# Wide products for eight chunk pairs, grouped seam splits and a narrower last column block in a one-core fp32 transformer layer

## Chip, core and metric

One core of a Trainium2 chip runs the whole layer as one program. The metric is the device time of one execution in microseconds; the lower the better. The engines named below are TensorE (PE, with its weight loads PEld), VectorE (DVE), ScalarE (ACT), GpSimd (POOL) and SyncE (SP, which issues most DMAs).

## What is computed

The reference is one decoder layer on 256 tokens of width 1024, in fp32. Each of its four blocks normalises its input by RMS, adds the normalised output to the residual x, and has its own gains:

```
x = x + 0.5 * rmsnorm(swiglu(rmsnorm(x), w_gate, w_up, w_down))      # FFN 1, inner width 2816
proj = rmsnorm(x) @ w_in                       # q, k, v (8 heads of 64) and 512 pool channels
y = concat(attention(q, k, v), pool(p_in)) @ w_out                    # the mixer
x = x + rmsnorm(y)
c = cross_attention(rmsnorm(x) @ wq, rmsnorm(mem) @ wkv) @ wo         # 256 memory rows, 4 heads of 256
x = x + rmsnorm(c)
x = x + 0.5 * rmsnorm(swiglu(...))                                    # FFN 2
```

With 256 tokens the attention of the mixer is plain causal attention with a linear bias; the pool branch takes trailing means over 2, 4, 8 and 16 positions.

## The kernel before

**Products.** Every large product is made from three products of rounded halves. A weight block `w` of 128x128 is split into `hi` (a rounding copy on ACT, L76) and `lo = w - hi` (DVE, L77), and the activations are split in the same way, `X[:, k, :256]` being the high part of feature block k for all 256 tokens and `X[:, k, 256:]` the low part. The product is `lo*Xhi + hi*Xhi + hi*Xlo`.

- `pair` (L206) makes two output chunks of 128 features by 256 tokens in the two halves of one PSUM bank. It calls `product` (L176) eight times per chunk, once per k: three matmuls of 256 columns (L179 to L181), each with a weight load of its own.
- `gate_up` (L593), used in the two FFNs, makes a chunk in a bank of its own. Per k it runs `lo` over the 256 columns of Xhi into the second half of the bank (L603) and `hi` over all 512 columns of X into the whole bank (L606). The two halves are then added: ACT copies the second half to `cmb` (L611), DVE adds it to the first half (L612) into an SBUF tile.
- `group` makes four chunks at once, k by k: four `lo` matmuls (L233) and then for each chunk L238 and L240. `rows` makes token-major rows of 512 columns (L266 to L268).

**Weights.** All weight blocks stand in DRAM in the order of use, eight blocks to a unit (1 MB for two units). `Weights.get` (L125) hands out blocks; when a new unit u begins it first makes the splits (L76, L77) of all units up to u + LEAD, with LEAD = 4, unless the list `pace` says another number for this unit. A split made further ahead is queued earlier on ACT and DVE.

**Order.** PE runs in program order everywhere. Between `seam(True)` and `seam(False)` all engines run in program order; elsewhere a scheduler at build time orders ACT, DVE, POOL and SP. The two seams of the change are those from FFN 1 to the mixer and from the mixer to the cross-attention, both by `row_end` (L378). A seam runs, in this order:

1. `products` (L391): sets `pace`, takes the last three weight units, finishes the row products of both token halves (`row_sums`), adds the first half to the residual, and transposes it on PE into two banks.
2. `middle` (L416): the root of the second half; eight high parts (`x_hi`, ACT, L384) of the first half; residual additions (L357); eight low parts (`x_lo`, DVE, L388).
3. Two filler chunks (a `pair` of the memory keys K), each followed by `turned(i)` (L433): four transposes of the second half into one bank, then for each of the four blocks `x_hi` and `x_lo`.
4. `group` on the new activations (four chunks, four units: G0 to G3, two k per unit). Its `before(j)` adds the evacuation of the filler pair (`k_flush`) at k = 1 and squares for the next norm at k = 2, 4, 6 and 7.

The old pace is four units ahead for the first two units of `products`, three for its third, two for the two fillers and for G0, and three for G1 and G2.

**After the first seam (mixer).** `pair` of k (chunks 4, 5), the root `x_root` and its broadcast `x_spread` (PE L292), `q_out` (L1000, multiplies the four q chunks and the k chunk pair by the norm), `pair` (6, 7), scores of heads 0 to 3, `pool_pair(3)` (L1010), scores of heads 4 to 7, `pool_pair(1)`, four steps of `rows` for v with the transposes of the attention probabilities (`self_turn`, L787 to L790) and the pool products (`pool_out`, L830) between them, then a K pair. `pool_windows` begins with the multiply L813 on DVE, which reads the pool chunk's bank; POOL then makes the sums. Softmax of the scores runs on DVE and ACT.

**After the second seam (cross-attention).** Two `pair`s of wq (chunks 4 to 7), a K pair, `k_flush`, and then scores against the memory with the v rows between them.

**PSUM.** Eight banks: two under the name `small`, six under `accum`. Each `pair` takes one `accum` bank until what it feeds has read it; a `self_turn` of heads 0 to 3 takes one each, the v rows two, a `pool_out` one each.

**Tail.** `last_rows` (L718) finishes FFN 2. For the second token half the first 256 output columns go by PE: x times the identity (L736) plus y times a diagonal of the norm (L741), copied out by ACT (L745) and stored by ACT's queue (L748). The columns 512 to 1023 and 256 to 511 go by DVE (L753) and SP (L746, L747).

Of the kernel before, what the change touches and what calls it, by code (L numbers as in the profile page):

```python
# [15 lines left out]
P = 128  # L16
# [126 lines left out]
def build(nc, io, tiles_only=False):  # L143
# [53 lines left out]
    def chunk(name, X, nk, col, evac, alloc=accum):  # L197
# [5 lines left out]
            evac(ps)  # L203
        pr.add(run, [(name, k * P, col) for k in range(nk)])

    def pair(name, X, cols, done, between=None, alloc=accum):  # L206

        names = [name] * 2 if isinstance(name, str) else name
        box = []

        def half(s):
            def run():
                if s == 0:
                    box.append(alloc())
                for k in range(ND):
                    product(halves(box[0])[s], st["w"].get(), st[X][:, k, :], s == k == 0, k == ND - 1)
                if s:
                    done(box[0])
# [159 lines left out]
    def row_end(parts, ks, weights, factor, nxt, pre, fillers):  # L378
# [4 lines left out]
        def x_hi(t, c):  # L383
            nc.scalar.activation(st[nxt][:, c, t * P:(t + 1) * P], st["turned", t, c], AF.Copy, scale=gain(pre, c))  # L384
# [5 lines left out]

        def products():  # L391
            st["w"].pace = [(LEAD, None)] * (LATE - 1)
            st["w"].pace += [(LEAD - 1, None)] + [(LEAD - 2, None)] * 3 + [(LEAD - 1, None)] * 2 if fillers else []
            ws = [st["w"].get(UNIT) for _ in ks]
            st["w"].flush()
            st["ys"] = keep([P, 2, D], "y")
            r = row_root(row_sums(parts, ks, ws, 0, factor))
            st[nxt] = xsplit()
            st["xsum"] = tmp([P, 2, 2], "xsum")
            for d in HALVES:  # L400
                row_add(0, d, r)
            box["later"] = []
            between = {} if fillers else {(1, i): lambda i=i: turn_first(i) for i in range(2)}
            box["sums"] = row_sums(parts, ks, ws, 1, factor, box["later"], between)
            if fillers:
                for i in range(2):
                    x_turn(0, range(4 * i, 4 * i + 4), small)
# [25 lines left out]
        def turned(i):  # L433
            def run():
                cs = range(4 * i, 4 * i + 4)
                x_turn(1, cs, accum)
                for c in cs:
                    x_hi(1, c)
                    x_lo(1, c)
            return run  # L440

# [148 lines left out]
    def ffn(n, X, before, aside, last):  # L590
        wg, wu, wd = (f"ffn{n}_w_{s}" for s in ("gate", "up", "down"))

        def gate_up(f, done):  # L593

            box = []

            def half(s):
                def run():
                    ps = (accum, small)[s]()
                    for k in range(0, ND, 2):  # L600
                        ws = [st["w"].get() for _ in range(2)]
                        for i, (hi, lo) in enumerate(ws):
                            nc.tensor.matmul(ps[:, S:], lo, st[X][:, k + i, :S], start=k == i == 0, stop=False,  # L603
                                             skip_group_check=True)
                        for i, (hi, lo) in enumerate(ws):
                            nc.tensor.matmul(ps, hi, st[X][:, k + i, :], start=False, stop=k + i == ND - 1,  # L606
                                             skip_group_check=True)
                    if s == 0:
                        box.append(st["ffn"].tile([P, 2, S], F32, name="gu", bufs=6))
                    c = tmp([P, S], "cmb")  # L610
                    nc.scalar.copy(c, ps[:, S:])  # L611
                    nc.vector.tensor_tensor(box[0][:, s, :], ps[:, :S], c, op=ALU.add)  # L612
                    if s:
                        done(box[0])
                return run
            return [(half(s), [(w, k * P, f * P) for k in range(ND)]) for s, w in enumerate((wg, wu))]
# [101 lines left out]
    def last_rows(parts, ks, weights):  # L718
        def run():
            ws = [st["w"].get(UNIT) for _ in ks]  # L720
            st["w"].flush()
            ys = st["ys"] = keep([P, 2, D], "y")
            xt = st["xt"]
            for t in range(2):
                o = io["out"][t * P:(t + 1) * P, :]
                later = [] if t else None
                s = row_sums(parts, ks, ws, t, 0.5, later)
                if t == 0:
                    r = row_root(s)
                    for i in range(4):  # L730
                        row_out(t, quarter(i), r)
                    for a, b in ((0, 512), (512, 1024)):
                        nc.sync.dma_start(o[:, a:b], ys[:, t, a:b])
                    continue
                turn = accum()
                nc.tensor.matmul(turn[:, :S], st["ident"], xt[:, t, quarter(0)], start=True, stop=False,  # L736
                                 skip_group_check=True)
                r = row_root(s, later[0])
                diag = tmp([P, P], "diag", bufs=1)
                nc.scalar.activation(diag, st["ident"], AF.Copy, scale=r)  # L740
                nc.tensor.matmul(turn[:, :S], diag, ys[:, t, quarter(0)], start=False, stop=True,  # L741
                                 skip_group_check=True)
                for d in (slice(512, 1024), quarter(1)):
                    row_out(t, d, r)
                nc.scalar.copy(ys[:, t, quarter(0)], turn[:, :S])  # L745
                nc.sync.dma_start(o[:, 512:], ys[:, t, 512:])  # L746
                nc.sync.dma_start(o[:, S:512], ys[:, t, S:512])  # L747
                nc.scalar.dma_start(o[:, :S], ys[:, t, :S])  # L748
        pr.add(run, weights)

    def row_out(t, d, r):
# [212 lines left out]
        pr.add = add  # L964
        return out

    K = [collect(pair, "xa_wkv", "xs_mem", [c * P, (c + 1) * P], k_out(c)) for c in range(0, ND, 2)]
    V = [s for half in range(2)
         for s in rows("xa_wkv", "xs_mem", D + 512 * half, xv_done(512 * half))]
    vv = rows("w_in", "xs_mix", D, v_done)  # L970
# [22 lines left out]

    group("w_in", "xs_mix", [c * P for c in range(4)], lambda ps: held.update(q=ps), before=run)
    seam(False)
    pair("w_in", "xs_mix", [4 * P, 5 * P], lambda ps: held.update(k=ps), lambda: side(x_root))
    table(AF.Exp)
    side(x_spread)

# [10 lines left out]
    def pool_pair(g):  # L1010
        def done(ps):
            for i in (g, g - 1):
                pool_in(i)(halves(ps)[g - i])
                pool_windows(i)
        pair("w_in", "xs_mix", [(12 + g) * P, (11 + g) * P], done)
    side(q_out)
    pair("w_in", "xs_mix", [6 * P, 7 * P], lambda ps: scaled_pair("qk", 6, ps))
    side(self_scores, 0, small)
    side(self_scores, 1, accum)
    pool_pair(3)  # L1020
# [59 lines left out]
    side(xq_root)  # L1080
    table(AF.Exp)
    for c in (4, 6):
        pair("xa_wq", "xs_xa", [c * P, (c + 1) * P], lambda ps, c=c: split_pair(st["xs_q"], c, ps))
    k = K.pop(0)
    pr.add(*k[0])
    pr.add(*k[1])
# [139 lines left out]
```

## Time and profile before

| | |
|---|---|
| median of 3 runs | 573.33 us (573.03 to 573.44) |
| the profiled execution's own time | 573.43 us |
| its span, first to last instruction | 571.6 us |
| mean granted PE clock | 0.998 |
| PE busy | 562.0 us, 98% of the span |
| DVE, ACT busy | 408.0 us (71%), 343.6 us (60%) |
| POOL busy | 15.7 us |
| DMA | 107.02 MB, mean 187 GB/s |

The span leaves about 1.8 us of the execution's time outside. Times of rows are microseconds from the start of the span. A row of the timeline is start, duration, engine, line, operation, output<-inputs, shape, count of merged instructions, and in brackets the idle time before it and what ended it. Consecutive matmuls overlap in their recorded durations, so the rate of PE is read from the distance between starts.

### The profile page before, as it was taken

How to read it: one execution, taken by the hardware profiler on the slowest of the kernel's cores; microseconds unless marked ns; L12 is line 12 of the kernel's file. 1: busy time of each engine (PE TensorE's matmuls, PEld its weight loads, DVE VectorE, ACT ScalarE, POOL GpSimd, SP SyncE). 2: the span in 40 equal slices, each digit the busy share in tenths (PEclk: the TensorE clock that was granted, in tenths of full speed). 3: DMA queues.
4: the chain of work that ended last, by engine and by line, in shares of the span. 5: the costliest groups of instructions: out<-in, count | busy, mean ns of one | idle time of the engine just before them, and what ended most of it. 6: DMA issues, size and time to landing. Idle time of an engine off the chain costs nothing.

```text
span 571.6 us, 8375 instructions
## 1 busy us (share of the span) xinstructions
PE 562.0 (98%) x3264; PEld 492.7 (86%) x3264; DVE 408.0 (71%) x661; ACT 343.6 (60%) x615; POOL 15.7 (3%) x34
## 2 busy tenths in 40 slices
PE   9999999999999999999999999999999999999996
PEld 8888888888888989988889988888888888888884
DVE  5989667777875678985478666466976776767644
ACT  7788665556556585884369456358754555555542
POOL 0000000000000000550000000000000000000000
PEclk9999999999999999999999999999999999999999
DMA  8996866555541378262077644332866556564102
GB/s 298 365 357 236 303 242 214 198 211 163 215 163 61 109 282 309 75 221 75 0 257 294 225 147 148 108 113 77 337 218 215 162 208 201 171 215 159 66 0 73
DMA packets 29255, 107.02 MB, mean 187 GB/s; under 512 B 2080, under 2 KB 2976, under 8 KB 28832
## 3 DMA queue, kind: packets, MB, share of 16 engines
q1 hardware_dynamic: 28640, 106.01, 52.3%
q10 hardware_dynamic: 576, 0.48, 0.3%
q8 instruction: 25, 0.41, 0.3%
q14 instruction: 14, 0.11, 0.1%
HBM read 105.44 MB, written 1.05 MB: 186 GB/s over the span
## 4 chain that ended last, share of the span: by engine, by line
PE 89%; DVE 6%; ACT 2%; DMA 2%; issue 1%; SPq 0%; DVEq 0%; ACTq 0%
PE sm L606 12%; PE acc L606 12%; PE acc L306 10%; PE acc L304 10%; PE acc L305 9%; PE acc L603 6%; PE sm L603 6%; PE acc L179 3%; PE acc L180 3%; PE acc L181 3%; DVE wlo L77 2%; PE acc L266 2%; PE acc L268 2%; PE acc L267 2%; DMA wraw<-w 2%; DVE xs L388 1%
## 5 line engine op out<-in xcount | busy, mean ns | idle before, releaser
L77 DVE TENSOR_TENSOR wlo<-wraw,whi 128x1024 fp32r<-128x1024 f32 x184 | 224.9, 1230 | 71.4 <-ACT whi L76 70.3
L76 ACT CAST whi<-wraw 128x1024 fp32r<-128x1024 f32 x184 | 191.7, 1052 | 48.6 <-PE acc L306 37.2
L606 PE MATMUL acc<-xs,whi 128*128 128x512 f32 x320 | 100.5, 395 | 0.0
L606 PE MATMUL sm<-xs,whi 128*128 128x512 f32 x320 | 100.5, 395 | 0.0
L603 PEld LDWEIGHTS acc<-xs,wlo 128*128 128x128 f32 x320 | 60.0, 188 | 14.5 <-DVE wlo L77 0.8
L603 PEld LDWEIGHTS sm<-xs,wlo 128*128 128x128 f32 x320 | 59.8, 188 | 13.8
L306 PE MATMUL acc<-whi,h 128*128 128x512 f32 x176 | 68.6, 390 | 0.2 <-DVE h L195 0.2
L304 PE MATMUL acc<-whi,h 128*128 128x512 f32 x176 | 68.6, 390 | 0.0
L305 PE MATMUL acc<-wlo,h 128*128 128x512 f32 x176 | 68.5, 389 | 0.0
L603 PE MATMUL acc<-xs,wlo 128*128 128x256 f32 x320 | 63.0, 278 | 0.6 <-DVE wlo L77 0.6
L603 PE MATMUL sm<-xs,wlo 128*128 128x256 f32 x320 | 63.2, 279 | 0.0
L606 PEld LDWEIGHTS sm<-xs,whi 128*128 128x128 f32 x320 | 48.7, 189 | 0.0
L606 PEld LDWEIGHTS acc<-xs,whi 128*128 128x128 f32 x320 | 48.7, 189 | 0.0
L179 PE MATMUL acc<-xs,wlo 128*128 128x256 f32 x160 | 46.1, 288 | 0.0
L180 PE MATMUL acc<-xs,whi 128*128 128x256 f32 x160 | 45.2, 283 | 0.0
L181 PE MATMUL acc<-xs,whi 128*128 128x256 f32 x160 | 45.2, 283 | 0.0
L611 ACT COPY cmb<-acc 128x256 f32<-128x256 f32 x40 | 14.9, 372 | 49.7 <-PE acc L606 49.7
L611 ACT COPY cmb<-sm 128x256 f32<-128x256 f32 x40 | 14.9, 372 | 49.2 <-PE sm L606 48.9
L306 PEld LDWEIGHTS acc<-whi,h 128*128 128x128 f32 x176 | 33.0, 188 | 7.7 <-DVE h L195 0.9
L305 PEld LDWEIGHTS acc<-wlo,h 128*128 128x128 f32 x176 | 33.0, 188 | 7.0
L304 PEld LDWEIGHTS acc<-whi,h 128*128 128x128 f32 x176 | 33.0, 188 | 7.0
L179 PEld LDWEIGHTS acc<-xs,wlo 128*128 128x128 f32 x160 | 30.6, 191 | 0.3
(196 smaller groups left out, 883.5 us busy)
## 6 DMA issues: line engine op xcount, KB each, us to landing
wraw<-w SPq DMA_DIRECT2D x91, 1024.0 KB, 4.9
post<-post SPq DMA_DIRECT2D x4, 512.0 KB, 5.2
wraw<-w SPq DMA_DIRECT2D x7, 256.0 KB, 5.7
wraw<-w SPq DMA_DIRECT2D x2, 512.0 KB, 7.1
y<-memt SPq DMA_DIRECT2D x1, 1024.0 KB, 5.2
y<-mem SPq DMA_DIRECT2D x1, 1024.0 KB, 7.0
xt<-xt SPq DMA_DIRECT2D x1, 1024.0 KB, 6.8
out_dram<-y SPq DMA_DIRECT2D x3, 256.0 KB, 2.1
```

What stands on the lines that cost most here:

```text
L76: self.nc.scalar.copy(hi, raw)
L77: eng.tensor_tensor(lo, raw, hi.bitcast(F32), op=ALU.subtract)
L179: nc.tensor.matmul(o, lo, X[:, :S], start=first, stop=False, skip_group_check=True)
L180: nc.tensor.matmul(o, hi, X[:, :S], start=False, stop=False, skip_group_check=True)
L181: nc.tensor.matmul(o, hi, X[:, S:], start=False, stop=last, skip_group_check=True)
L266: nc.tensor.matmul(box[t], a, hi, start=k == 0, stop=False)
L304: nc.tensor.matmul(o, a, hi, start=first, stop=False, skip_group_check=True)
L305: nc.tensor.matmul(o, a, lo, start=False, stop=False, skip_group_check=True)
L306: nc.tensor.matmul(o, b, hi, start=False, stop=last, skip_group_check=True)
L603: nc.tensor.matmul(ps[:, S:], lo, st[X][:, k + i, :S], start=k == i == 0, stop=False, skip_group_check=True)
L606: nc.tensor.matmul(ps, hi, st[X][:, k + i, :], start=False, stop=k + i == ND - 1, skip_group_check=True)
L611: nc.scalar.copy(c, ps[:, S:])
```

## The change

Five edits.

1. `wide`, `wide_chunk` and `wide_pair` are new. `wide_chunk` is the body of `gate_up` taken out: per two k it runs two `lo` matmuls of 256 columns and two `hi` matmuls of 512, then ACT copies the second half to `cmb` and DVE adds. `wide_pair` makes two such chunks, each in an `accum` bank of its own, into one SBUF tile `wide` of 512 columns with one buffer, and hands that tile to what read the bank before.
2. Eight `pair`s become `wide_pair`s: K chunks (2, 3) and (6, 7), w_in chunks (4, 5), (6, 7), (15, 14) and (13, 12), wq chunks (4, 5) and (6, 7). The two K pairs that fill the seams stay `pair`s.
3. In `turned` the four `x_hi` come first and then the four `x_lo`.
4. The pace of a seam is three units ahead for five units (third unit of `products`, both fillers, G0, G1), then the default four.
5. In the tail the block that goes by PE is 128 columns wide; DVE takes columns 128 to 511; the store of ACT's queue is issued in the program before that of SP's columns 128 to 511.

```diff
+    def wide(ps, ws, Xs, first, last):
+        for i, (hi, lo) in enumerate(ws):
+            nc.tensor.matmul(ps[:, S:], lo, Xs[i][:, :S], start=first and i == 0, stop=False, skip_group_check=True)
+        for i, (hi, lo) in enumerate(ws):
+            nc.tensor.matmul(ps, hi, Xs[i], start=False, stop=last and i == 1, skip_group_check=True)
+
+    def wide_chunk(X, ps, o):
+        for k in range(0, ND, 2):
+            wide(ps, [st["w"].get() for _ in range(2)], [st[X][:, k + i, :] for i in range(2)], k == 0, k == ND - 2)
+        c = tmp([P, S], "cmb")
+        nc.scalar.copy(c, ps[:, S:])
+        nc.vector.tensor_tensor(o, ps[:, :S], c, op=ALU.add)
+
+    def wide_pair(name, X, cols, done, between=None):
+        box = []
+        def half(s):
+            def run():
+                if s == 0:
+                    box.append(tmp([P, 2 * S], "wide", bufs=1))
+                wide_chunk(X, accum(), box[0][:, s * S:(s + 1) * S])
+                if s:
+                    done(box[0])
+            return run
...
@@ products
-            st["w"].pace += [(LEAD - 1, None)] + [(LEAD - 2, None)] * 3 + [(LEAD - 1, None)] * 2 if fillers else []
+            if fillers:
+                st["w"].pace += [(LEAD - 1, None)] * 5
@@ turned
                 for c in cs:
                     x_hi(1, c)
+                for c in cs:
                     x_lo(1, c)
@@ last_rows
-                nc.tensor.matmul(turn[:, :S], diag, ys[:, t, quarter(0)], start=False, stop=True,
+                nc.tensor.matmul(turn[:, :P], diag, ys[:, t, :P], start=False, stop=True,
...
-                for d in (slice(512, 1024), quarter(1)):
+                for d in (slice(512, 1024), slice(P, 512)):
                     row_out(t, d, r)
-                nc.scalar.copy(ys[:, t, quarter(0)], turn[:, :S])
+                nc.scalar.copy(ys[:, t, :P], turn[:, :P])
                 nc.sync.dma_start(o[:, 512:], ys[:, t, 512:])
-                nc.sync.dma_start(o[:, S:512], ys[:, t, S:512])
-                nc.scalar.dma_start(o[:, :S], ys[:, t, :S])
+                nc.scalar.dma_start(o[:, :P], ys[:, t, :P])
+                nc.sync.dma_start(o[:, P:512], ys[:, t, P:512])
@@ schedule
-    K = [collect(pair, ...) for c in range(0, ND, 2)]
+    K = [collect(wide_pair if c in (2, 6) else pair, ...) for c in range(0, ND, 2)]
-    pair("w_in", "xs_mix", [4 * P, 5 * P], ...)        # and [6, 7], pool_pair, xa_wq (4, 6)
+    wide_pair("w_in", "xs_mix", [4 * P, 5 * P], ...)
```

## Rows read from the trace of the kernel before

**Rows 1.** The page's busy times by engine, over the whole span.
```profile
PE 562.0 (98%) x3264; PEld 492.7 (86%) x3264; DVE 408.0 (71%) x661; ACT 343.6 (60%) x615; POOL 15.7 (3%) x34
```

**Rows 2.** The longest entry of the waits of PE, whole span: what for, us in total, times, longest.
```profile
PE acc L233 <- DVE wlo L77: 2.6, 2, 1.3
```

**Rows 3.** Timeline of PE, the `lo` matmuls of the group behind the first seam: both k of G0, the first k of G2 and of G3, and the first matmul behind the group; then the first matmuls of the group behind the second seam and behind that group.
```profile
198.65 0.72 PE L233 MATMUL acc<-xs,wlo 128*128 128x256 f32 x4
200.17 0.64 PE L233 MATMUL acc<-xs,wlo 128*128 128x256 f32 x4
...
206.06 0.75 PE L233 MATMUL acc<-xs,wlo 128*128 128x256 f32 x4 [1.29 <-DVE wlo L77]
...
209.03 0.64 PE L233 MATMUL acc<-xs,wlo 128*128 128x256 f32 x4
...
211.91 0.28 PE L179 MATMUL acc<-xs,wlo 128*128 128x256 f32 x1
...
292.08 0.72 PE L233 MATMUL acc<-xs,wlo 128*128 128x256 f32 x4
...
305.36 0.28 PE L179 MATMUL acc<-xs,wlo 128*128 128x256 f32 x1
```

**Rows 4.** Timeline of ACT and then of DVE in the first seam: the first two high parts of the second token half and the high half of G1; the low parts of the first half, the first low part of the second half, and the splits of G1 and G2.
```profile
195.62 0.37 ACT L384 ACTIVATE xs<-acc,gain 128x128 fp32r<-128x128 f32 x1 [1.11 <-PE acc L363]
197.44 0.37 ACT L384 ACTIVATE xs<-acc,gain 128x128 fp32r<-128x128 f32 x1 [1.45 <-DVE xs L388]
...
199.28 1.04 ACT L76 CAST whi<-wraw 128x1024 fp32r<-128x1024 f32 x1
...
195.00 2.15 DVE L388 SCALAR_TENSOR_TENSOR xs<-sm,gain,xs 128x128 fp32r<-128x128 f32 x8
197.07 0.34 DVE L388 SCALAR_TENSOR_TENSOR xs<-acc,gain,xs 128x128 fp32r<-128x128 f32 x1
...
200.35 1.23 DVE L77 TENSOR_TENSOR wlo<-wraw,whi 128x1024 fp32r<-128x1024 f32 x1 [0.58 <-ACT whi L76]
...
204.78 1.23 DVE L77 TENSOR_TENSOR wlo<-wraw,whi 128x1024 fp32r<-128x1024 f32 x1 [0.58 <-ACT whi L76]
```

**Rows 5.** Timeline of ACT and DVE in the seam to FFN 2, where four high parts stand together and then four low parts.
```profile
385.40 1.14 ACT L384 ACTIVATE xs<-sm,gain 128x128 fp32r<-128x128 f32 x4 [1.17 <-PE sm L363]
386.57 1.13 DVE L388 SCALAR_TENSOR_TENSOR xs<-sm,gain,xs 128x128 fp32r<-128x128 f32 x4 [0.98 <-ACT xs L384]
```

**Rows 6.** Timeline of PE: the first matmul of the last `pair` chunk before the cross-attention scores and the first matmul behind it; then the first matmul of a `gate_up` chunk of FFN 2 and that of the second chunk after it.
```profile
319.75 0.28 PE L179 MATMUL acc<-xs,wlo 128*128 128x256 f32 x1
...
322.63 0.28 PE L845 MATMUL xsc<-xk,xs 128*128 128x256 f32 x1
...
392.51 0.40 PE L603 MATMUL acc<-xs,wlo 128*128 128x256 f32 x2
...
398.08 0.40 PE L603 MATMUL acc<-xs,wlo 128*128 128x256 f32 x2
```

**Rows 7.** Groups by line and form, whole span (count | busy us, mean ns | idle before): the copy and the addition of a `gate_up` chunk, a multiply of 512 columns out of SBUF; and the waits of that copy (from the view of waits).
```profile
L611 ACT COPY cmb<-acc 128x256 f32<-128x256 f32 x40 | 14.9, 372 | 49.7 <-PE acc L606 49.7
L612 DVE TENSOR_TENSOR gu<-acc,cmb 128x256 f32<-128x256 f32 x40 | 16.9, 424 | 19.1 <-ACT cmb L611 19.1
L624 DVE TENSOR_TENSOR gu<-gu,rBx 128x512 f32<-128x512 f32 x40 | 27.6, 691 | 1.1
ACT cmb L611 <- PE sm L606: 48.9, 35, 2.4
```

**Rows 8.** Busy time by stretch (length, then PE, PEld, DVE, ACT, POOL with counts, PE clock, DMA share, GB/s): the mixer's softmax stretch.
```profile
226.00:246.00 20.00, 20.00 (x148) 18.52 (x148) 19.99 (x64) 13.10 (x41) 10.03 (x20) 1.00 0.25 90
```

**Rows 9.** Timeline of the mixer behind the scores: a weight split and the last pool multiply on DVE, ACT's copies of the first two transposed heads, and on PE the fourth head's transposes, the first two pool products, and the first `pair` chunk of K.
```profile
241.43 1.21 DVE L77 TENSOR_TENSOR wlo<-wraw,whi 128x1024 fp32r<-128x1024 f32 x1
...
244.68 0.41 DVE L813 TENSOR_TENSOR pin<-acc,rBx 128x256 f32<-128x256 f32 x1
...
246.45 0.85 ACT L790 COPY ps<-acc 128x384 f32<-128x384 f32 x2
...
245.23 0.27 PE L787 MATMUL acc<-const,ps 128*128 128x128 f32 x1
...
248.30 1.03 PE L830 MATMUL acc<-pin,poolw 128*128 128x256 f32 x4
...
252.51 0.36 PE L179 MATMUL acc<-xs,wlo 128*128 128x256 f32 x1
```

**Rows 10.** Timeline of the tail, all engines and queues from the root of the last rows on, and the time from issue to landing of the two 128 KB stores (count, KB each, us).
```profile
566.97 1.15 DVE L753 SCALAR_TENSOR_TENSOR y<-y,fs,xt 128x512 f32<-128x512 f32 x2
567.43 0.70 PE L741 MATMUL acc<-y,diag 128*128 128x256 f32 x2 [1.58 <-ACT diag L740]
568.16 0.37 ACT L745 COPY y<-acc 128x256 f32<-128x256 f32 x1 [0.79 <-PE acc L741]
568.19 0.37 SPq L747 DMA_DIRECT2D out_dram<-y  x1
568.57 0.35 ACTq L748 DMA_DIRECT2D out_dram<-y  x1
out_dram<-y SPq DMA_DIRECT2D x1, 128.0 KB, 2.2
out_dram<-y ACTq DMA_DIRECT2D x1, 128.0 KB, 2.1
```

More of the change, by code (lines that the diff above doesn't have):

```diff
@@ L204, in chunk @@
         pr.add(run, [(name, k * P, col) for k in range(nk)])
+    def wide(ps, ws, Xs, first, last):
[19 more added lines that the diff above has]
+            return run
+        for s in range(2):
+            pr.add(half(s), [(name, k * P, cols[s]) for k in range(ND)])
+            if between and not s:
+                between()
     def pair(name, X, cols, done, between=None, alloc=accum):
@@ L599, in run @@
                     ps = (accum, small)[s]()
[L600 to L607, printed above, removed]
                     if s == 0:
                         box.append(st["ffn"].tile([P, 2, S], F32, name="gu", bufs=6))
-                    c = tmp([P, S], "cmb")
-                    nc.scalar.copy(c, ps[:, S:])
-                    nc.vector.tensor_tensor(box[0][:, s, :], ps[:, :S], c, op=ALU.add)
+                    wide_chunk(X, ps, box[0][:, s, :])
                     if s:
@@ L735, in run @@
                 turn = accum()
-                nc.tensor.matmul(turn[:, :S], st["ident"], xt[:, t, quarter(0)], start=True, stop=False,
+                nc.tensor.matmul(turn[:, :P], st["ident"], xt[:, t, :P], start=True, stop=False,
                                  skip_group_check=True)
@@ L965, in collect @@
         return out
-    K = [collect(pair, "xa_wkv", "xs_mem", [c * P, (c + 1) * P], k_out(c)) for c in range(0, ND, 2)]
+    K = [collect(wide_pair if c in (2, 6) else pair, "xa_wkv", "xs_mem", [c * P, (c + 1) * P], k_out(c))
+         for c in range(0, ND, 2)]
     V = [s for half in range(2)
@@ L995, in build @@
     seam(False)
-    pair("w_in", "xs_mix", [4 * P, 5 * P], lambda ps: held.update(k=ps), lambda: side(x_root))
+    wide_pair("w_in", "xs_mix", [4 * P, 5 * P], lambda ps: held.update(k=ps), lambda: side(x_root))
     table(AF.Exp)
@@ L1014, in done @@
                 pool_windows(i)
-        pair("w_in", "xs_mix", [(12 + g) * P, (11 + g) * P], done)
+        wide_pair("w_in", "xs_mix", [(12 + g) * P, (11 + g) * P], done)
     side(q_out)
-    pair("w_in", "xs_mix", [6 * P, 7 * P], lambda ps: scaled_pair("qk", 6, ps))
+    wide_pair("w_in", "xs_mix", [6 * P, 7 * P], lambda ps: scaled_pair("qk", 6, ps))
     side(self_scores, 0, small)
@@ L1082, in build @@
     for c in (4, 6):
-        pair("xa_wq", "xs_xa", [c * P, (c + 1) * P], lambda ps, c=c: split_pair(st["xs_q"], c, ps))
+        wide_pair("xa_wq", "xs_xa", [c * P, (c + 1) * P], lambda ps, c=c: split_pair(st["xs_q"], c, ps))
     k = K.pop(0)
```

## The prediction

> **What bounds the kernel now.** I read the busy times by engine first: PE is busy for 562.0 of 571.6 us and no other engine above 71% [rows 1]. A recorded matmul overlaps the next, so "busy" alone proves little; the waits of PE say how much is really lost. Their longest entry is 2.6 us in two waits for a low weight half [rows 2]; these are the two seams. So the time is the length of PE's own stream plus a few stalls, and an edit gains only where it shortens that stream, removes one of these stalls, or shortens the tail behind PE's last row product. Next I read the distances between starts in PE's timeline [rows 3, 6], then ACT and DVE in the seam [rows 4], then the one stretch in which DVE has no slack: from 226 to 246 us it is busy for 19.99 of 20.00 us [rows 8].
>
> **Wide products.** A chunk by `pair` takes 322.63 - 319.75 = 2.88 us of PE [rows 6]. The same work by `gate_up`'s form, two chunks from 392.51 to 398.08, takes 5.57 / 2 = 2.785 us [rows 6]. The columns streamed are the same; one matmul and one weight load of three per k are gone. Sixteen chunks at 0.095 us: **-1.5 us**, all on PE and so all on the path. The price is the nearest one there is, the same code on the same shapes; the bounds are 1.4 and 1.6 by the rounding of the starts.
>
> The Trainium skill, "TensorE: Matmul & The Clock Gate", section "Back-to-back issue gap", states for an isolated matmul at full clock a distance of columns / 2.4 GHz plus about 2.5 ns; by it the 128 matmuls removed would be worth about 0.3 us, as an estimate. The rows above show 0.095 us for a chunk, or 12 ns for each matmul removed, so the trace speaks against that page here.
>
> Each wide chunk adds one copy on ACT (0.372 us) and one addition on DVE (0.424 us) [rows 7]: 16 of each, 6.0 us on ACT and 6.8 us on DVE. What read the bank (512 columns, 0.69 us for a multiply that reads SBUF [rows 7]) now reads the SBUF tile; I price that as no change, since the additions, which read a bank, cost no less per column. Outside 226 to 246 us PE's stream hides them. Inside it four pool chunks add 4 x 0.424, and the addition of chunk 7 stands just ahead: 2.1 us on a DVE that is full. DVE may start that stretch as much earlier as PE does (1.7 us by the first seam and four chunks of 0.095, 2.0 us), so I expect its end where it was, while PE arrives at the work behind it 1.66 + 8 x 0.095 = 2.4 us earlier. What is late next is a PSUM bank: the v rows hold two `accum` banks and the transposes of heads 0 to 3 hold four, so the first two pool products need ACT's copies of heads 0 and 1, which end at 246.45 + 0.85 = 247.30 [rows 9]. PE now begins these products at 248.30 [rows 9]; 2.4 us earlier is 245.9, up to 1.4 us too early for the second bank and about 1.0 for the first. The scheduler is free to place the copies earlier, ahead of what waits for DVE, in which case it costs nothing. Bounds 0 and 1.4; the old order lies nearer the middle than either end, since one of the two banks is free by half a copy sooner: **+0.6 us**.
>
> **Seams.** The group behind the first seam runs from 198.65 to 211.91, 13.26 us for four units; G3, which waits for nothing, takes 211.91 - 209.03 = 2.88 [rows 3], so four would take 11.52. The excess is 1.74, of which 0.08 is the restart behind the transposes (200.17 - 198.65 against 1.44). That leaves 1.66. The second group, 305.36 - 292.08 = 13.28, leaves 1.68 [rows 3]. The cause stands in the ACT and DVE rows: the high part at 195.62 is alone, the next comes at 197.44 because it waits for a low part, and that low part had to wait for the eight low parts of the first half, begun at 195.00 [rows 4]. From there ACT and DVE alternate at about 0.78 us a block, and the splits of G1 and G2 stand behind four blocks each in their queues; G2's low half ends at 204.78 + 1.23 = 206.01 and PE starts at 206.06 [rows 3, 4].
>
> Two edits act on this. Four together take 1.14 us on ACT and 1.13 on DVE where the code already has them so [rows 5]. And with three units ahead G1's split is queued before the first `turned`, G2's before the second, G3's at the start of the group. Put in order: ACT sits idle for 1.11 us before 195.62 [rows 4], and G1's high half (1.04 us [rows 4]) fills just that; its low half follows the low parts of the first half at 197.1 and ends at 198.3, against the 201.5 at which PE wants it. The four low parts then end at 199.4 and G2's low half at 200.6, against 204.4. The first low part of the second half, which G0 needs at 199.3, moves from 197.4 to 198.6 and is still in time by 0.7. What is moved: the DMA of the next raw pair is issued by G2's split, so on SP it now stands before the load of the gains of the next norm instead of behind it; both are far ahead of their use. The whole excess goes: **-3.3 us**, bounds 0 and -3.4. What is late next is the pair behind the group, and its splits move up as well.
>
> **Tail.** The block by PE, ACT and ACT's store ends last: 567.43 (0.70 us of matmuls), copy 568.16, issue 568.57, landing 2.1 us later [rows 10]. With half the columns I take 0.2 off the matmuls and 0.1 off the copy. SP's last store (issued 568.19, landing in 2.2 us [rows 10]) has 384 columns instead of 256 and waits for a DVE operation some 0.07 longer, so it lands about 0.3 before the old end and becomes the last. **-0.25 us**, bounds 0 and -0.35.
>
> **Sum.** The profiled execution took 573.43 us, 0.1 above the median 573.33. 573.43 - 1.5 + 0.6 - 3.3 - 0.25 = 568.98: **569.0 us**. The kernel's measurement can tell about 0.2% (1.15 us) from no change.
>
> **Rivals.**
> - *The mixer gives PE's lead back.* In the kernel before, the bank of the last pool pair was released by the multiply that ends at 244.68 + 0.41 = 245.09, and the transposes of the fourth head start at 245.23 [rows 9], 0.14 us later. If the new additions of the pool chunks are queued as late as that multiply, PE waits there for most of its 2.4 us. For it: DVE has no gap there [rows 8]. Against it: the addition no longer waits for what follows it, and each chunk has a bank of its own. The loss is 1.2 to 2.4 instead of 0.6: 569.6 to 570.8. Chance 22%.
> - *The seam is cured by half.* ACT and DVE might keep alternating, if the wait comes from reading one bank by both rather than from the order of the code, or the earlier splits push the low parts behind PE's need. The low parts have 0.7 us of room only. Against it: four together do run unhindered elsewhere [rows 5]. Half of 3.3 lost gives 570.6, all of it 572.3. Chance 10%.
> - *The wide form saves only the page's gap*, 0.3 us: that would need PE to run these chunks differently from `gate_up`'s, and ends at 570.2. Chance 3%.
> - *Slower: chunk copies stop ACT's queue.* Each copy waits for PE at the head of ACT, up to 2.4 us in the FFNs [rows 7], with the splits behind it. The split at 241.43 on DVE ends at 242.64 and, counted by units of eight blocks, is first used at 252.51 [rows 9]: 9.9 us of room, 7.5 with PE 2.4 earlier. The eight copies ahead of it could hold ACT for 8 x 2.4 = 19 us; from 7.5 us on PE waits, and 12 us beyond that give 568.4 + 12, about 580. Against it: in the FFNs the same copies stop no split that PE waits for (the only longer waits of PE are at the seams [rows 2]). Chance 4%.
>
> **How the numbers follow.** The forecast, with 0 to 1.2 us lost in the mixer (568.3 to 569.6), gets 58%; 3% are left for more than I count (wider tail gain, fewer restarts), below 567.9. The range **567.9 to 571.0** takes in the forecast, the first rival, the page's rival and half of the second. Faster by over 0.2% (below 572.2): all but the last rival and a part of the second, 0.93; within 0.2%: 0.03; slower: 0.04.
>
> **What would show it.** Right: the starts of the group's units in both seams 2.88 us apart with no wait for a low half; four high and four low parts in blocks of 1.14; chunks of 2.785 us at eight pairs; PE at the first two pool products 1.5 to 2.4 us earlier than 248.3; ACT's store issued near 568.25 on the old scale. Wrong: a wait of PE at the pool products, at the fourth head's transposes or at the K chunk of over 1.2 us; a new wait at the start of the group; chunks still at 2.88.

## The result and the profile after

The changed kernel takes **569.41 us** (median of 4 runs, 569.15 to 570.64) against 573.38 of the kernel before on the same chip: ratio 0.9934, interval 0.9917 to 0.9951, 3.97 us less. The prediction said 569.0 (567.9 to 571.0). The profiled execution is the longest of the four, 570.64 us with a span of 568.83. In it PE waited 0.51 us for the high half of FFN 1's first weights, and its matmuls of 256 columns then started 0.21 us apart instead of 0.12 until 10.3 us (why is not shown; the granted clock in these rows is 1.00). From 34 us on it is 1.27 us behind the trace of before. I therefore compare stretches between the two traces, not their ends.

Busy times by engine [rows 1], and all entries of the waits of PE [rows 2]: what for, us in total, times, longest.

```profile
PE 561.1 (99%) x3136; PEld 486.6 (86%) x3136; DVE 410.0 (72%) x677; ACT 346.8 (61%) x631; POOL 19.7 (3%) x34
```
```profile
PE acc L765 <- ACT diag L764: 1.8, 1, 1.8
PE warm L541 <- DVE cmb L538: 1.2, 1, 1.2
PE acc L270 <- ACT whi L108: 0.5, 1, 0.5
PE acc L854 <- POOL pin L849: 0.5, 1, 0.5
```

The wait for low halves in the groups is gone. L765 and L541 stand in the kernel before too (1.6 and 1.2 us), and L270 is the late start. L854 is new: PE waits for a pool window of GpSimd. (Lines of the old code that are named here stand 24 to 34 lines further down, the group's `lo` matmul at L265, `x_hi` at L416, `x_lo` at L420, the pool products at L854.)

**Seams.** Timeline of PE, the first `lo` matmuls of G0 to G3 of the first group and the first matmul behind it; then the second group's start, its end, and the end of the six chunks behind it [rows 3, 6].

```profile
199.93 0.72 PE L265 MATMUL acc<-xs,wlo 128*128 128x256 f32 x4
...
202.88 0.64 PE L265 MATMUL acc<-xs,wlo 128*128 128x256 f32 x4
...
205.76 0.64 PE L265 MATMUL acc<-xs,wlo 128*128 128x256 f32 x4
...
208.64 0.64 PE L265 MATMUL acc<-xs,wlo 128*128 128x256 f32 x4
...
211.52 0.40 PE L209 MATMUL acc<-xs,wlo 128*128 128x256 f32 x2
...
291.62 0.72 PE L265 MATMUL acc<-xs,wlo 128*128 128x256 f32 x4
...
303.21 0.40 PE L209 MATMUL acc<-xs,wlo 128*128 128x256 f32 x2
...
319.94 0.28 PE L869 MATMUL xsc<-xk,xs 128*128 128x256 f32 x1
```

From the second on the units stand 2.88 us apart (the first, with the restart behind the transposes, takes 2.95). The groups take 11.59 us each, 1.67 and 1.69 less than before: **-3.36 us**. The six wide chunks take 319.94 - 303.21 = 16.73 us, 2.79 each instead of 2.88.

ACT and then DVE in the first seam [rows 4]; with 1.27 taken off, the times compare with those of the prediction.

```profile
195.63 1.09 ACT L76 CAST whi<-wraw 128x1024 fp32r<-128x1024 f32 x1
196.90 1.15 ACT L416 ACTIVATE xs<-acc,gain 128x128 fp32r<-128x128 f32 x4 [0.17 <-PE acc L395]
197.91 1.06 ACT L76 CAST whi<-wraw 128x1024 fp32r<-128x1024 f32 x1
```
```profile
196.27 2.15 DVE L420 SCALAR_TENSOR_TENSOR xs<-sm,gain,xs 128x128 fp32r<-128x128 f32 x8
198.34 1.22 DVE L77 TENSOR_TENSOR wlo<-wraw,whi 128x1024 fp32r<-128x1024 f32 x1
199.47 1.12 DVE L420 SCALAR_TENSOR_TENSOR xs<-acc,gain,xs 128x128 fp32r<-128x128 f32 x4
200.51 1.22 DVE L77 TENSOR_TENSOR wlo<-wraw,whi 128x1024 fp32r<-128x1024 f32 x1
```

G1's low half ends at 199.56 - 1.27 = 198.3 as foretold, the four low parts at 199.3 (199.4), G2's low half at 200.5 (200.6).

**Mixer.** POOL, then DVE, then PE around the last pool products [rows 9].

```profile
243.62 7.57 POOL L846 TENSOR_TENSOR win<-pin 128x271 f32<-128x271 f32 x1 [3.27 <-DVE pin L837]
...
253.72 1.62 POOL L849 TENSOR_TENSOR pin<-win,aw 128x256 f32<-128x256 f32 x1
```
```profile
243.13 0.75 DVE L837 TENSOR_TENSOR pin<-wide,rBx 128x256 f32<-128x256 f32 x2
243.79 6.90 DVE L77 TENSOR_TENSOR wlo<-wraw,whi 128x1024 fp32r<-128x1024 f32 x6
```
```profile
247.25 1.03 PE L854 MATMUL acc<-pin,poolw 128*128 128x256 f32 x4
...
254.33 0.59 PE L854 MATMUL acc<-pin,poolw 128*128 128x256 f32 x2
255.38 0.70 PE L854 MATMUL acc<-pin,poolw 128*128 128x256 f32 x2 [0.46 <-POOL pin L849]
255.73 0.59 PE L209 MATMUL acc<-xs,wlo 128*128 128x256 f32 x2
```

The same in the kernel before: on POOL the like of the long addition and the last window, on PE the last two pool products and the chunk behind them.

```profile
243.18 0.68 POOL L822 TENSOR_TENSOR win<-pin 128x271 f32<-128x271 f32 x1 [1.75 <-DVE pin L813]
...
249.62 1.60 POOL L825 TENSOR_TENSOR pin<-win,aw 128x256 f32<-128x256 f32 x1
```
```profile
255.47 1.02 PE L830 MATMUL acc<-pin,poolw 128*128 128x256 f32 x4
256.14 0.47 PE L179 MATMUL acc<-xs,wlo 128*128 128x256 f32 x1
```

The first two pool products start at 247.25, 1.05 us earlier than [rows 9] on the clock of the trace and 2.32 on PE's own: nothing is lost up to there. At the last two, PE's next chunk starts at 255.73 where 255.01 was due (254.33 plus the 0.67 that the products take in the kernel before): **+0.72 us**. One window addition lasts 7.57 us. Additions of the same shape take 0.64 to 0.68 where no split runs beside them. It begins just ahead of six weight splits on DVE without a gap and ends 0.5 us behind the last. The last window, at 253.72, again falls on a split and ends at 255.34.

**Tail.** ACT's copy and the two last stores, and the stores' KB and us from issue to landing [rows 10].

```profile
565.16 0.27 ACT L769 COPY y<-acc 128x128 f32<-128x128 f32 x1 [0.58 <-PE acc L765]
565.46 0.38 ACTq L771 DMA_DIRECT2D out_dram<-y  x1
565.49 0.33 SPq L772 DMA_DIRECT2D out_dram<-y  x1
```
```profile
out_dram<-y SPq DMA_DIRECT2D x1, 192.0 KB, 2.2
...
out_dram<-y ACTq DMA_DIRECT2D x1, 64.0 KB, 2.4
```

Counted from the diagonal's start (L764, 564.18), ACT's store is issued at 1.28 us instead of 1.60. It lands 2.4 us later instead of 2.1 and is still the last to land, behind SP's. To the end of the span it is 4.65 us; before it was 4.68.

### The profile page after: what moved, and what is told of

Same layout as the page of the kernel before. It is cut to its first block, busy times and chain, and to the rows that moved or that the text cites. A ratio compares the mean times of both kernels' runs of the same rounds, so it can differ in the third digit from the quotient of the medians.

```text
span 568.8 us, 8167 instructions
## 1 busy us (share of the span) xinstructions
PE 561.1 (99%) x3136; PEld 486.6 (86%) x3136; DVE 410.0 (72%) x677; ACT 346.8 (61%) x631; POOL 19.7 (3%) x34
## 3 DMA queue, kind: packets, MB, share of 16 engines
HBM read 105.44 MB, written 1.05 MB: 187 GB/s over the span
## 4 chain that ended last, share of the span: by engine, by line
PE 89%; DVE 5%; POOL 2%; issue 1%; DMA 1%; ACT 1%; POOLq 0%; DVEq 0%; SPq 0%; ACTq 0%
PE acc L211 16%; PE sm L211 12%; PE acc L338 10%; PE acc L336 10%; PE acc L337 10%; PE acc L209 8%; PE sm L209 6%; PE acc L270 2%; PE acc L272 2%; PE acc L265 2%; POOL win L846 2%; PE acc L298 1%; PE acc L300 1%; PE acc L299 1%; DVE wlo L77 1%
## 5 line engine op out<-in xcount | busy, mean ns | idle before, releaser
L211 PE MATMUL acc<-xs,whi 128*128 128x512 f32 x448 | 140.7, 395 | 0.0
L209 PEld LDWEIGHTS acc<-xs,wlo 128*128 128x128 f32 x448 | 83.7, 188 | 19.1
L209 PE MATMUL acc<-xs,wlo 128*128 128x256 f32 x448 | 88.6, 279 | 0.0
L211 PEld LDWEIGHTS acc<-xs,whi 128*128 128x128 f32 x448 | 68.2, 189 | 0.0
L218 ACT COPY cmb<-acc 128x256 f32<-128x256 f32 x56 | 20.8, 371 | 67.2 <-PE acc L211 67.1
L219 DVE TENSOR_TENSOR gu<-acc,cmb 128x256 f32<-128x256 f32 x40 | 17.0, 424 | 19.9 <-ACT cmb L218 19.9
L219 DVE TENSOR_TENSOR gu<-sm,cmb 128x256 f32<-128x256 f32 x40 | 17.0, 424 | 17.5 <-ACT cmb L218 17.5
L648 DVE TENSOR_TENSOR gu<-gu,rBx 128x512 f32<-128x512 f32 x40 | 27.6, 691 | 1.1
L270 PE MATMUL acc<-xs,whi 128*128 128x256 f32 x96 | 25.4, 295 | 0.5 <-ACT whi L108 0.5
```

The source lines that it names most:

```text
L209: nc.tensor.matmul(ps[:, S:], lo, Xs[i][:, :S], start=first and i == 0, stop=False, skip_group_check=True)
L211: nc.tensor.matmul(ps, hi, Xs[i], start=False, stop=last and i == 1, skip_group_check=True)
L219: nc.vector.tensor_tensor(o, ps[:, :S], c, op=ALU.add)
L270: nc.tensor.matmul(o[i], hi, st[X][:, k, :S], start=first and i % 2 == 0, stop=False, skip_group_check=True)
L648: nc.vector.tensor_tensor(t, src, st["rBx"][:, None, :].to_broadcast([P, 2, S]), op=ALU.mult)
```

## The experiments

My theory after the comparison: the seams and the chunks paid as worked out; the loss in the mixer is no bank but GpSimd's windows, put late by the wide form and shut out by DVE's splits; the tail's gain is eaten by its landing. The last column is the change against before in medians, with the ratio and its interval.

| run | what | us | against before |
|---|---|---|---|
| e_wide | before + wide pairs | 572.82 | -0.53; 0.9990 (0.9981 to 1.0000) |
| e_seam | before + order + pace | 570.14 | -3.21; 0.9946 (0.9931 to 0.9961) |
| e_order | before + order | 569.81 | -3.54; 0.9939 (0.9924 to 0.9953) |
| e_pace | before + pace | 569.76 | -3.59; 0.9939 (0.9924 to 0.9954) |
| e_banks | before + two banks | 570.24 | -3.14; 0.9943 (0.9923 to 0.9962) |
| e_tail | before + tail | 573.28 | -0.10; 0.9997 (0.9988 to 1.0007) |
| e_poolorder | after, products moved | 568.68 | -4.70; 0.9915 (0.9900 to 0.9930) |
| e_onein | after, other splits | 568.59 | -4.79; 0.9913 (0.9898 to 0.9928) |
| e_poolpair | after, old last pool pair | 568.70 | -4.63; 0.9920 (0.9903 to 0.9936) |
| e_probe | after + dummy additions | 569.36 | -3.97; 0.9931 (0.9911 to 0.9951) |
| e_store | after, stores cut at 256 | 569.27 | -4.11; 0.9927 (0.9910 to 0.9943) |
| e_best | after, moved, four more wide chunks | 568.36 | -4.97; 0.9913 (0.9898 to 0.9928) |

### Seams: which edit, and why they alternated

e_seam takes the new `turned` and the new pace, e_order the first alone, e_pace the second alone:

```diff
                 for c in cs:
                     x_hi(1, c)
+                for c in cs:
                     x_lo(1, c)
```
```diff
-            st["w"].pace += [(LEAD - 1, None)] + [(LEAD - 2, None)] * 3 + [(LEAD - 1, None)] * 2 if fillers else []
+            if fillers:
+                st["w"].pace += [(LEAD - 1, None)] * 5
```

> The kernel before with the new order of the low parts and the new pace of the splits, nothing else. My theory: both groups run their four units 2.88 us apart with no wait for a low half, 1.66 us less in each seam, 3.3 us in all. Rival (cured by half): one wait of 0.7 to 1.3 us stays in each group, 1.6 us in all. Whether the lead of 1.66 us survives the mixer: if the wait for the last pool window in the changed kernel is set by the queues of DVE and GpSimd and not by PE's lead, it shows here too, and the gain falls to 2.6 us.

> The kernel before with the new order alone (four high parts, then four low parts); the splits keep their old pace, so G1's stands behind the first four blocks and G2's behind the second four. My theory (the queues were stretched by the alternation): four blocks take 1.15 us instead of about 3.1 on either engine, G1's low half then ends near 199.4 and G2's near 201.7 on the scale of before, ahead of the 201.5 and 204.4 at which PE wants them; so the order alone brings the whole 1.66 us a seam, 3.3 us in all. Rival (it is the place of the splits in the queue): the 1.3 us waits stay wholly or by half, 0 to 1.6 us in all.

> The kernel before with the new pace alone (splits three units ahead); high and low parts still alternate. My theory: G1's split now stands ahead of the first four blocks and G2's ahead of the second four, so G1's low half ends near 198.3 and G2's near 203.5, both ahead of PE's need at 201.5 and 204.4; the low parts of the second four come at about 204.3 and 205.1, just in time. So the pace alone would bring nearly all, 2.6 to 3.3 us. Rival (the alternating parts now become late themselves): PE waits for low parts of the blocks instead, and the gain is 0 to 1.6 us.

All three run both groups in 11.6 us; in each trace PE is 1.67 us earlier behind the first group than ahead of it, and 1.68 behind the second. The first part of the lead comes through the mixer whole: e_seam starts its chunk behind the last pool products 1.65 us before the old time, and there is no wait for a window. So either edit alone is worth the whole 3.3 us, and the second adds nothing. What differs between the three profiled runs (570.02, 569.95 and 569.72 us) is PE's start in FFN 1, by up to 0.4 us, not the seams.

ACT and DVE of e_order: the four parts together make G1's low half (198.05) and G2's (201.10) early enough without the new pace.

```profile
195.57 1.15 ACT L384 ACTIVATE xs<-acc,gain 128x128 fp32r<-128x128 f32 x4 [1.11 <-PE acc L363]
196.59 1.06 ACT L76 CAST whi<-wraw 128x1024 fp32r<-128x1024 f32 x1
```
```profile
197.02 1.12 DVE L388 SCALAR_TENSOR_TENSOR xs<-acc,gain,xs 128x128 fp32r<-128x128 f32 x4
198.05 1.22 DVE L77 TENSOR_TENSOR wlo<-wraw,whi 128x1024 fp32r<-128x1024 f32 x1
...
201.10 1.22 DVE L77 TENSOR_TENSOR wlo<-wraw,whi 128x1024 fp32r<-128x1024 f32 x1
```

ACT and DVE of e_pace still alternate, but G1's low half now stands ahead of the blocks (196.66) and G2's between them (201.07).

```profile
195.21 0.37 ACT L384 ACTIVATE xs<-acc,gain 128x128 fp32r<-128x128 f32 x1 [0.17 <-PE acc L363]
198.17 0.37 ACT L384 ACTIVATE xs<-acc,gain 128x128 fp32r<-128x128 f32 x1 [2.59 <-DVE xs L388]
```
```profile
196.66 1.21 DVE L77 TENSOR_TENSOR wlo<-wraw,whi 128x1024 fp32r<-128x1024 f32 x1
197.79 0.34 DVE L388 SCALAR_TENSOR_TENSOR xs<-acc,gain,xs 128x128 fp32r<-128x128 f32 x1
...
201.07 1.23 DVE L77 TENSOR_TENSOR wlo<-wraw,whi 128x1024 fp32r<-128x1024 f32 x1 [0.58 <-ACT whi L76]
```

Why the old order alternated at all was the prediction's second rival: one bank read by both engines, or the order of the code. e_banks keeps the old order and pace:

```diff
-                x_turn(1, cs, accum)
+                x_turn(1, cs[::2], accum)
+                x_turn(1, cs[1::2], accum)
```

> The kernel before with the old order and the old pace, but the four transposes of the second token half go to two banks by turns (blocks 0 and 2, blocks 1 and 3). Theory A (ACT's next high part waits because DVE reads the same bank for the low part): neighbours no longer wait for each other, four blocks take some 1.6 us instead of 3.1, PE's wait in each group goes wholly or by half. Theory B (the wait comes from the order of the code, or from the tile that both write): ACT and DVE go on alternating at 0.78 us a block, PE waits 1.3 us in both groups, same time as before. More banks in use could also cost PE a wait for one.

Theory A, and more than half of it: neighbours now go in twos, and only the third block waits, for the low part that reads its bank. PE's wait is gone in both groups (1.67 and 1.68 us less).

```profile
195.62 0.63 ACT L384 ACTIVATE xs<-acc,gain 128x128 fp32r<-128x128 f32 x2 [0.88 <-PE acc L363]
197.65 0.62 ACT L384 ACTIVATE xs<-acc,gain 128x128 fp32r<-128x128 f32 x2 [1.41 <-DVE xs L388]
```
```profile
197.28 0.60 DVE L388 SCALAR_TENSOR_TENSOR xs<-acc,gain,xs 128x128 fp32r<-128x128 f32 x2
198.05 0.61 DVE L388 SCALAR_TENSOR_TENSOR xs<-acc,gain,xs 128x128 fp32r<-128x128 f32 x2 [0.18 <-ACT xs L384]
```

So in this program the waits exist because a bank has one reader at a time, in the order of the code, and that order only decides how often the reader changes. (A bank is one tile of the program here, so these runs cannot tell the bank from the tile.) The Trainium skill gives a rule that fits, on the page "PSUM — Partial Sum Buffer", section "PSUM bank collisions raise a hardware error": ScalarE and VectorE may not read the same bank in the same partitions at once, even in other columns. These traces agree in that no two such reads overlap; no run here tried to let them.

### Wide chunks and the mixer

e_wide is the changed kernel with the old `turned`, the old pace and the old tail put back.

> The kernel before with the eight wide pairs alone; both seams and the tail as before. My theory (a matmul and a weight load saved per k, PE's stream shorter by 0.085 to 0.095 us a chunk): a chunk start to start 2.785 to 2.80 us instead of 2.88, 16 chunks, and both seams keep their wait of 1.3 us for a low weight half: 1.3 to 1.5 us less than before in all. In the mixer PE comes some 1.7 us later than in the changed kernel, so it should find the last pool window ready and lose nothing there. Rival (only the 2.5 ns of a matmul's gap is saved): 0.3 us. Rival (the copies and additions hold up the queues of ACT and DVE): a new wait of PE in the mixer, and no gain or a loss.

Half a miss. The chunks paid: in its trace PE gains 0.72 us over nine chunks up to the last pool products, 0.07 on the tenth and 0.55 on the six behind the second seam, 1.34 in all or 0.084 a chunk. But it too lost 0.72 us at the last pool products, with a lead of only 0.70 us there, where e_seam with a lead of 1.67 lost nothing. PE's lead is therefore not the cause; the loss comes with the wide form.

e_poolpair and e_poolorder ask how:

```diff
-        wide_pair("w_in", "xs_mix", [(12 + g) * P, (11 + g) * P], done)
+        (pair if g == 1 else wide_pair)("w_in", "xs_mix", [(12 + g) * P, (11 + g) * P], done)
```
```diff
     pr.add(*k[0])
+    pr.add(*k[1])
     side(pool_out, 1)
     side(pool_out, 0)
-    pr.add(*k[1])
```

> The changed kernel with the last pool pair alone back in the old form (one bank, the multiply by the norm reads PSUM, no copy and no addition). My theory: the wait at the last pool product comes from where the wide form puts the two multiplies on DVE, at 243.13 right ahead of six weight splits; in the old form they come 1 to 2 us earlier and the window additions get done alongside. So the 7.57 us addition is gone, the wait of 0.72 us with it, against 0.17 us more for two chunks: 568.9. Rival (the other wide chunks ahead of it cause it, by filling ACT and DVE): the wait stays, 569.6.

> The changed kernel with one thing moved: the last two pool products stand behind the second chunk of the K pair instead of between its two chunks. My theory: the 0.72 us that PE loses there is a wait for the last pool window alone (it ends at 255.33, PE would then come near 257.1), so the wait goes and the run is 0.7 us shorter than the changed kernel, 568.7 against 569.4. Rival (PE is held there by a bank, or by ACT and DVE): the loss stays or shows at the transposes of the last two heads, 0 to 0.3 us shorter.

Both came out as expected, 568.70 (568.9) and 568.68 (568.7). In e_poolpair the two multiplies run at 239.40 and 241.47, and three of the windows' additions are done before the splits begin at 243.12. (The 243.13 of the changed kernel stands in a trace that runs 1.3 us late. In e_poolorder, which has the same form and an ordinary start, the two multiplies stand together at 241.79 and the splits begin at 242.46. So the old form moves the first multiply 2.4 us and the second 0.6 us ahead, and the splits back by 0.7.) In e_poolorder the long addition is still there (242.28, 7.57 us), but PE comes at 255.81, behind the last window:

```profile
242.28 7.57 POOL L846 TENSOR_TENSOR win<-pin 128x271 f32<-128x271 f32 x1 [3.27 <-DVE pin L837]
...
252.37 1.65 POOL L849 TENSOR_TENSOR pin<-win,aw 128x256 f32<-128x256 f32 x1
```
```profile
255.81 1.02 PE L854 MATMUL acc<-pin,poolw 128*128 128x256 f32 x4
```

Two more runs ask what stretches the addition. e_onein makes the low halves in that stretch from one operand, so that this part of its product is no longer the reference's; e_probe puts one dummy addition beside each of 52 splits in FFN 1, far from the pool branch:

```diff
...
+        if self.plain:
+            eng.tensor_scalar(lo, raw, 1.0, None, op0=ALU.mult)
+        else:
             eng.tensor_tensor(lo, raw, hi.bitcast(F32), op=ALU.subtract)
...
```
```diff
+        if 8 <= u < 60:
+            self.nc.gpsimd.tensor_tensor(self.probe[:, :256], raw[:, :256], hi[:, :256].bitcast(F32), op=ALU.add)
         eng.tensor_tensor(lo, raw, hi.bitcast(F32), op=ALU.subtract)
...
```

> The changed kernel, but the low weight halves made between the last pool pair and the K pair (six to eight of them) are a multiplication of the raw half by 1 instead of raw minus high half, so those DVE instructions read one SBUF operand instead of two; these low halves then hold the whole weight, that part of the product is changed. Theory 1 (the GpSimd window addition of 7.57 us is shut out by DVE instructions that read two SBUF operands): it falls to about 0.7 us, the last window is ready some 5 us earlier, PE's wait of 0.72 us goes, 568.7 us. Theory 2 (any run of DVE instructions shuts it out): it lasts as long as the run does. Theory 3 (the addition waits for something else that ends near 251.2): it stays at about 7.6 us.

> The changed kernel with a dummy GpSimd addition (128x256, both operands in SBUF) for each of 52 weight units in FFN 1, released by the same high half as DVE's split of that unit, so that the two engines start together; nothing reads what it writes. Theory 1 (one of the two engines is shut out while the other's instruction with two SBUF operands runs): when both start together, the addition takes its own 0.6 us or 0.6 plus the rest of the split, up to 1.8, or else the split takes 1.2 plus 0.6; no pair overlaps without loss. Theory 2 (they share bandwidth or do not meet): both stay within some tens of ns of 0.6 and 1.22 us. Time: within 0.5 us of the changed kernel.

e_onein decides little on this. The time is what theory 1 expected, but the scheduler also put the first window addition at 240.59, ahead of the splits, so that the case it was to test did not arise. Beside the one-operand instructions two GpSimd operations took 0.93 and 1.06 us instead of 0.74 and 0.61 (the first of them also met a multiply with two SBUF operands). What it does show: with every wide pair in place its windows are done at 246.07 and PE loses nothing. So the wide form need not cost the 0.72 us; the order that the scheduler makes of it counts.

e_probe decides for theory 1 as far as single splits go. POOL, then DVE, for two pairs:

```profile
60.16 1.71 POOL L78 TENSOR_TENSOR margin<-wraw,whi 128x256 f32<-128x256 f32 x1 [4.00 <-ACT whi L76]
...
96.29 0.87 POOL L78 TENSOR_TENSOR margin<-wraw,whi 128x256 f32<-128x256 f32 x1 [1.07 <-ACT whi L76]
```
```profile
60.05 1.23 DVE L79 TENSOR_TENSOR wlo<-wraw,whi 128x1024 fp32r<-128x1024 f32 x1 [0.52 <-ACT whi L76]
...
96.48 1.76 DVE L79 TENSOR_TENSOR wlo<-wraw,whi 128x1024 fp32r<-128x1024 f32 x1
```

Where the split starts 0.1 us ahead it takes its 1.23 us and the addition 1.71; where the addition starts first (0.02 us are enough in one pair) it mostly takes 0.74 to 0.88 and the split up to 1.80. The later one waits for the whole of the earlier. The Trainium skill says this on the page "SBUF — State Buffer", section "Who interferes with whom": a VectorE instruction with two SBUF inputs and a GpSimd instruction that reads SBUF exclude each other for a whole instruction, and the first to issue wins; these pairs agree.

What stays open is why one addition had to wait for six splits. It lasted 7.56 or 7.57 us in all six kernels in which it began just ahead of them, and ended 0.5 us behind the last; that the splits held it is read from these times. In the kernel before and in e_poolpair a GpSimd operation got its turn after one split of a run (it lasted 1.6 to 1.8 us), and in e_probe too: the addition of 28.73 came between two splits in a row (from 28.62, 2.90 us for both instead of 2.4). In the changed kernel the addition began while the second multiply, with two SBUF operands in the wide form, was still running; that this decides it was not tried.

### Tail

e_tail is the kernel before with edit 5 alone; e_store is the changed kernel with the last two stores cut at column 256:

```diff
-                nc.scalar.dma_start(o[:, :P], ys[:, t, :P])
-                nc.sync.dma_start(o[:, P:512], ys[:, t, P:512])
+                nc.scalar.dma_start(o[:, :S], ys[:, t, :S])
+                nc.sync.dma_start(o[:, S:512], ys[:, t, S:512])
```

> The kernel before with the tail part 128 wide alone. The prediction's step: 0.25 us less, bounds 0 and 0.35. The profile of the changed kernel says rather 0 to 0.1: ACT's store is issued 0.31 us sooner behind the two matmuls, but took 2.4 us to land instead of 2.1. Rival (landing times of the stores vary by more than the gain): within 0.1 us of before, with landings from 2.0 to 2.4 us that have nothing to do with the width.

> The changed kernel with PE's part of the tail still 128 wide, but the last two stores cut at column 256 again, so ACT's store carries 128 KB in rows of 1 KB instead of 64 KB in rows of 512 bytes, and waits for ACT's copy and for DVE's part. It is issued at about the same time as in the changed kernel (1.3 us behind the start of the diagonal). Theory A (the store of 64 KB lands late, 2.4 us instead of 2.1, because of its short rows): it lands in 2.1 to 2.2 us and the tail from the diagonal to the end of the span falls from 4.62 to about 4.35. Theory B (it lands late because the other store is issued only 0.03 us behind it): still 2.4 us and 4.6.

e_tail cannot be told from no change. Landings did not vary at random, though: ACT's last store took 2.1 to 2.2 us in all six kernels with the old tail and 2.4 to 2.5 in all seven with the new, so that rival falls. Short rows are not the reason either; in e_store 128 KB in long rows landed as late:

```profile
out_dram<-y SPq DMA_DIRECT2D x1, 128.0 KB, 2.1
out_dram<-y ACTq DMA_DIRECT2D x1, 128.0 KB, 2.4
```

What all the late ones share is that SP's store is issued within 0.06 us of ACT's; with the old tail SP's went 0.38 us ahead. That fits theory B, but no run moved the issues apart alone, so the cause is not shown.

### A better version

e_best moves the pool products as in e_poolorder and makes the two K pairs inside the seams wide:

```diff
...
-    K = [collect(wide_pair if c in (2, 6) else pair, "xa_wkv", "xs_mem", [c * P, (c + 1) * P], k_out(c))
+    K = [collect(wide_pair, "xa_wkv", "xs_mem", [c * P, (c + 1) * P], k_out(c))
...
```

> The changed kernel with the last two pool products behind the second chunk of the K pair, and with the two K pairs that run inside the seams made wide as well (four more chunks, twenty in all). My theory: the move is worth the 0.72 us of the wait, four chunks at 0.085 us another 0.34 us: 568.3 to 568.4 against 569.4 of the changed kernel. Rival (the four extra copies on ACT and additions on DVE stand in the seams, where both queues are full, or their extra bank is wanted there): PE waits in one or both groups again, 569.0 to 570.5.

568.36 us (568.12 to 568.57), as my theory had it. That is below every run of the two kernels, though the interval of its ratio still overlaps that of the changed kernel. From e_poolorder it cannot be told by its times alone (ratios 0.9913 and 0.9915), but its trace shows the last 0.3 us: PE gains 0.16 us over the two fillers of the first seam and 0.16 over those of the second, 0.08 each, and both groups still take 11.6 us.

## Why the prediction was right, step by step

- **Seams, -3.3: right** (-3.36 in the trace, -3.21 in e_seam's median), and the order of events on ACT and DVE to 0.1 us. What the prediction had not seen: each of the two edits does it alone. Its rival, by which the alternation comes from one bank read by both engines, was right on the cause (e_banks) and wrong that this would keep the cure from working.
- **Wide, -1.5: nearly right.** 0.74 us over nine chunks, 0.09 on the tenth and 0.55 on six, 1.38 us in the trace, 0.086 a chunk instead of the 0.095 taken from `gate_up`'s two chunks. The estimate of 0.3 us from the figure that the Trainium skill gives for an isolated matmul ("TensorE: Matmul & The Clock Gate", section "Back-to-back issue gap") did not hold for this stream with a weight load to each matmul: e_wide's chunks saved 1.34 us, 128 matmuls at 10 ns.
- **Mixer, +0.6: right in size by luck, wrong in kind.** The step said that PE would arrive too early for a bank at the first two pool products, whose copies end at 247.30. The scheduler put these copies at 244.30, the case that the prediction named as costing nothing, and nothing was lost. The 0.72 us were lost at the last two products to GpSimd's window. The prediction priced the moved multiply "as no change" and did not follow whom it releases: a chain of GpSimd additions that had ended 4 us ahead of PE (251.22 against 255.47, in the trace of before) and that now met six splits in the order that the scheduler made. Its first rival, a bank held by the last pool pair at the fourth head, did not occur either (0.0 us there).
- **Tail, -0.25: too high.** ACT's store is issued 0.32 us sooner, as counted, but lands 0.3 us slower. What is left is 0.03 in the trace and 0.10, not told from none, in e_tail. The step took the old landing time for the new store and had SP's store land last; ACT's still does (565.46 + 2.4 against 565.49 + 2.2).
- **Sum.** -3.36 - 1.38 + 0.72 - 0.03 = -4.05, against -4.45 predicted and -3.97 measured in medians. The forecast is 0.4 us low because two gains, the wide chunks and the tail, were each set 0.1 to 0.2 too high, and the cost in the mixer 0.1 too low.

## What to carry to other kernels

When a wait sits in alternating queues of two engines, look for the shared buffer that makes them alternate, and try each remedy alone: here any one of three was enough. When an operation is moved, follow the engine that it releases, even one that is busy for 3% of the time; an idle engine can still be shut out by its neighbour just when its result is wanted. Price a store's landing as a thing of its own, not as the old figure scaled by size.

## What the runs showed of the hardware

- A DVE subtraction of 128x1024 with two operands in SBUF and a GpSimd addition with operands in SBUF did not overlap in e_probe: 1.23 and about 0.74 us for the one that starts first, up to 1.80 and 1.74 for the one that starts second. One addition that began just ahead of six such splits without a gap lasted 7.57 us, until 0.5 us behind the last; why it got no turn between them is open.
- A store on ACT's queue landed 0.3 us later (2.4 against 2.1 us) when SP's store was issued within 0.06 us of it (eight kernels) than when SP's went 0.38 us ahead (six), whether it carried 64 or 128 KB. No run shows that the issue times are the cause.
